# Reading the moving columns of a three-pass product in pairs, one from each half

## The chip, the cores and the metric

The kernel runs on one core of one Trainium2 chip. The metric is device time in microseconds (us), from the first to the last instruction of the program with what lies around it; less is better. The kernel before takes 2271.94 us as the median of three runs (2271.86 to 2279.43).

## The reference

A stack of four layers works on 256 tokens of width 1024, all in float32. Each layer is a half-step feed-forward block, a mixer and another half-step feed-forward block, each with an RMS norm before and after:

```python
for layer in range(DEPTH):
    g = norm_g[layer]
    h = swiglu_ffn(rms_norm(x, g[0]), ffn_w_gu[layer, 0], ffn_w_down[layer, 0])
    x = x + HALF_STEP * rms_norm(h, g[1])
    h = rms_norm(x, g[2])
    # layer % 3: 0 mLSTM, 1 RWKV-7, 2 retention; layers 0 and 3 are mLSTM
    h = mixer(h)
    x = x + rms_norm(h, g[3])
    h = swiglu_ffn(rms_norm(x, g[4]), ffn_w_gu[layer, 1], ffn_w_down[layer, 1])
    x = x + HALF_STEP * rms_norm(h, g[5])
```

`swiglu_ffn` is `(silu(x @ w_gate) * (x @ w_up)) @ w_down` with an inner width of 2816. Nearly all of the arithmetic is in its eight calls; the mixers add input products of 1024 x 3072 (mLSTM), 3 x 1024 x 1024 (RWKV) and 1024 x 6144 (retention), their output products, and their own recurrences in chunks.

## The kernel before, in words

The weights stream in as units of 128 x 2048 float32 (1 MB), in the order in which the products use them, all issued on SyncE's queue (`dma`). Each unit is split into a high and a low part both in float32r: ScalarE writes `hi` (L127), VectorE, or GpSimd in the mixers, writes `lo = raw - hi` (L135). Activations are split in the same way. A product is then three matmuls per block of 128 rows, high x high, high x low and low x high, summed in PSUM. The function `mm3` (L323) issues them, and it has two forms, after which operand moves through the array while the other is loaded into it as 128 x 128 weights:

- `w_moves=True` (L326 to L328): the weights move and the activations of 128 tokens are loaded. The result has tokens in its partitions and weight columns along the free dimension. The heads of all stages use it with 256 moving columns (`proj_B`, L349), so do the v, o and g products of the mixers, and the down and output products with 512 moving columns (`down_steps`, L376).
- `w_moves=False` (L330 to L332): the activations move, all 256 tokens of one block of 128 rows, and a block of 128 weight columns is loaded. The result is transposed: channels in the partitions, tokens along the free dimension. `proj_A` (L358) uses it for the feed-forward units after the head, `proj_qk` for the q and k of retention, `dense` of the mLSTM stage for its q and k, and `proj_unit` (L1446) of the RWKV stage for r and k.

In both forms the moving columns are read one after the other, as they lie in SBUF.

A feed-forward stage has 22 units of gate and up columns (each holds 128 gate and the 128 up columns of the same channels) and 11 of down rows. Its first three units are the head, computed token tile by token tile together with the end of the stage before; the other 19 go through `proj_A`, 48 matmuls of 256 columns each, and `evac_A` (L541). That function multiplies PSUM by the row of norm factors R (VectorE, L546), takes Silu of the gate half (ScalarE, L548), multiplies (VectorE, L549) and splits the result (L346, L347). After every second unit the down product of the chunk before runs, 24 matmuls of 512 columns, into four PSUM banks that hold the sum over the whole stage. Four further PSUM banks rotate for everything else. In these stages the order of the instructions is that of the code.

In the mLSTM and RWKV stages a planner (`Plan`) orders the instructions: each chain of steps yields an engine and an assumed cost in ns, and the planner issues what can start first on its clock. The retention stage is written out by hand. The lines that evacuate products of the second form there are L826 (mLSTM, times R), L1127 to L1129 (retention, rotation of q and k by cosine and sine) and L1526 (RWKV, copy on ScalarE).

The host lays out the weights before the launch (`a8` and `d2` from L2170 on, and the functions that put a stage's units in order). This takes no device time.

Of the kernel before, what the change touches and what calls it, by code (L numbers as in the profile page):

```python
# [20 lines left out]
P = 128  # L21
T = 256
# [12 lines left out]
class Net:  # L35
# [284 lines left out]
        s.nc.vector.tensor_copy(s.R, pt[:, :T])  # L320


    def mm3(s, out, wh, wl, ah, al, first, last, w_moves):  # L323
        mm = s.nc.tensor.matmul
        if w_moves:
            mm(out, ah, wh, start=first, stop=False)  # L326
            mm(out, ah, wl, start=False, stop=False)  # L327
            mm(out, al, wh, start=False, stop=last)  # L328
        else:
            mm(out, wh, ah, start=first, stop=False)  # L330
            mm(out, wh, al, start=False, stop=False)  # L331
            mm(out, wl, ah, start=False, stop=last)  # L332
# [16 lines left out]
    def proj_B(s, ps, unit, t):  # L349
# [5 lines left out]
        for k in range(NK):  # L355
            s.mm3(ps, wh[:, k, :], wl[:, k, :], s.xh[:, k, c], s.xl[:, k, c], k == 0, k == NK - 1, True)

    def proj_A(s, ps, unit, between=None):  # L358

        hi, lo = unit  # L360
        wh = hi.rearrange("p (k c) -> p k c", k=NK)
        wl = lo.rearrange("p (k c) -> p k c", k=NK)
        for g in range(2):
            c = slice(g * P, (g + 1) * P)
            for k in range(NK):
                s.mm3(ps[:, g * T:(g + 1) * T], wh[:, k, c], wl[:, k, c], s.xh[:, k, :], s.xl[:, k, :],
                      k == 0, k == NK - 1, False)
            if g == 0 and between is not None:
                between()
# [124 lines left out]
class Ffn(Stage):  # L494
# [46 lines left out]
    def evac_A(s, ps, u):  # L541
        n, nc = s.n, s.n.nc
        gn = n.sc(2, [2, T])
        sg = n.sc(1, [T])
        h = n.sc(1, [T])
        nc.vector.tensor_tensor(out=gn, in0=ps.rearrange("p (g t) -> p g t", g=2),  # L546
                                in1=n.R[:, None, :].to_broadcast([P, 2, T]), op=ALU.mult)
        nc.scalar.activation(out=sg, in_=gn[:, 0, :], func=AF.Silu)  # L548
        nc.vector.tensor_tensor(out=h, in0=gn[:, 1, :], in1=sg, op=ALU.mult)  # L549
        n.split([a[:, u % 2, :] for a in s.hTs(u // 2)], h)  # L550
# [147 lines left out]
class Mlstm(Stage):  # L698
# [66 lines left out]
    def dense(s):  # L765

        n, nc = s.n, s.n.nc
        yield "pe", 3000.0, True
        s.gates()
        s.plan.mark("gates")  # L770
        for i, (what, h) in enumerate(s.ORDER):
            yield from s.need(i)
            hi, lo = [u.rearrange("p (k c) -> p k c", k=NK) for u in n.get()]
            for j in range(2):
                c = slice(j * P, (j + 1) * P)
                for k in range(NK):
                    if k % 4 == 0:
                        yield "pe", 1300.0, j + k == 0
                        if j + k == 0:
                            ps = n.mm()  # L780
                    first, last = k == 0, k == NK - 1
                    if what == "qk":
                        n.mm3(ps[:, j * T:(j + 1) * T], hi[:, k, c], lo[:, k, c], n.xh[:, k, :], n.xl[:, k, :], first, last, False)
                    else:
                        n.mm3(ps[:, j * T:(j + 1) * T], hi[:, k, :], lo[:, k, :], n.xh[:, k, c], n.xl[:, k, c], first, last, True)
            n.free()
            s.ps[what, h] = ps.rearrange("p (g t) -> p g t", g=2)
            s.plan.mark("ps", what, h)
        yield from s.need(len(s.ORDER))
        yield [("y", 0), ("y", 1), ("hT", 0)]  # L790
        u = n.get()
        for t in range(2):
            if t == 0:
                n.load_gpost(s.gi)
                s.acc = n.new_acc()
            yield from n.down_steps(u, s.hT[0], t, s.acc[t], True, False)
        n.free()
# [20 lines left out]
    def conv(s):  # L818

        n, nc = s.n, s.n.nc  # L820
        for h in range(s.H):
            yield [("ps", "qk", h)]
            yield "ve", 600.0
            x = n.sc(4, [2, T + 3])
            nc.gpsimd.memset(x[:, :, 0:3], 0.0)
            nc.vector.tensor_tensor(out=x[:, :, 3:], in0=s.ps.pop(("qk", h)), in1=n.R[:, None, :].to_broadcast([P, 2, T]), op=ALU.mult)  # L826
            s.plan.drop()
            yield "po", 2220.0
            c = n.sc(4, [2, T])
            for g in range(2):  # L830
                nc.gpsimd.tensor_scalar(out=c[:, g, :], in0=x[:, g, 3:3 + T], scalar1=s.cw[:, 4 * g + h, 3:4], scalar2=None, op0=ALU.mult)
            for j in (2, 1, 0):
                yield "ve", 900.0
                for g in range(2):
                    nc.vector.scalar_tensor_tensor(out=c[:, g, :], in0=x[:, g, j:j + T], scalar=s.cw[:, 4 * g + h, j:j + 1],
                                                   in1=c[:, g, :], op0=ALU.mult, op1=ALU.add)
            yield "ac", 520.0, "sigmoid"
            sg = x[:, :, 0:T]
            nc.scalar.activation(out=sg, in_=c, func=AF.Sigmoid)
            yield "ve", 600.0  # L840
            s.qk[h] = n.sc(2, [2, T])
            nc.vector.tensor_tensor(out=s.qk[h], in0=c, in1=sg, op=ALU.mult)
            s.plan.mark("qk", h)

    def gates(s):
        n, nc = s.n, s.n.nc
        s.psg = n.mm()
        for k in range(NK):
            n.mm3(s.psg[0:36, 0:T], s.wgh[0][:, k, :], s.wgh[1][:, k, :], n.xh[:, k, :], n.xl[:, k, :], k == 0, k == NK - 1, False)
        n.make_R()  # L850

    def gates2(s):
# [190 lines left out]
class Retention(Stage):  # L1043
# [73 lines left out]
    def proj_qk(s, which, h):  # L1117
# [4 lines left out]
        if s.cos is not None and not hasattr(s, "nsin"):  # L1122
            n.make_R()
            s.rope()
        pv = ps.rearrange("p (g t) -> p g t", g=2)
        r, w = n.sc(2, [2, T]), n.sc(2, [2, T])
        nc.vector.tensor_tensor(out=r, in0=pv, in1=s.cos[:, None, :].to_broadcast([P, 2, T]), op=ALU.mult)  # L1127
        nc.vector.tensor_tensor(out=w[:, 0, :], in0=pv[:, 1, :], in1=s.nsin, op=ALU.mult)
        nc.vector.tensor_tensor(out=w[:, 1, :], in0=pv[:, 0, :], in1=s.sin, op=ALU.mult)  # L1129
        nc.gpsimd.tensor_tensor(out=r, in0=r, in1=w, op=ALU.add)  # L1130
        s.qk[which, h] = r
        n.ahead()
# [95 lines left out]
class Rwkv(Stage):  # L1228
# [200 lines left out]
                    s.plan.mark("ps", "v", i // 2, t)  # L1429
        s.plan.mark("V")  # L1430

    def unit(s):
        hi, lo = s.n.get()
        return hi.rearrange("p (k c) -> p k c", k=NK), lo.rearrange("p (k c) -> p k c", k=NK)

    def proj(s, hl, wh, wl, j, ps=None):

        for k in range(NK):
# [7 lines left out]
    def proj_unit(s, hl, name, g, j):  # L1446

        n = s.n
        yield from s.need(j)
        wh, wl = s.unit()  # L1450
        ps = None
        for j in range(2):
            c = slice(j * P, (j + 1) * P)
            ps = yield from s.proj(hl, wh[:, :, c], wl[:, :, c], j, ps)
        n.free()
        s.ps[name, g] = ps
        s.plan.mark("ps", name, g)
# [54 lines left out]
    def evacs(s):  # L1512
# [7 lines left out]
        for what in (("k", 0), ("k", 1), "la", "lg", ("r", 0), ("k", 2), ("k", 3), ("r", 1), ("r", 2), ("r", 3)):  # L1520
            if isinstance(what, tuple):
# [1 line left out]
                yield "ac", 500.0  # L1523
                store = s.kx if what[0] == "k" else s.r
                o = store[what[1]] = n.sc(2, [2, T])
                nc.scalar.activation(out=o.rearrange("p a b -> p (a b)"), in_=s.ps[what], func=AF.Copy)  # L1526
                s.plan.drop()
                s.plan.mark(*what)
                continue
# [82 lines left out]
    def lora2(s, i):  # L1612
# [6 lines left out]
        for g in range(4):  # L1619
            yield "pe", 640.0, True  # L1620
            ps = n.mm()
            for j in range(2):
                c = slice(D + (2 * g + j) * P, D + (2 * g + j + 1) * P)
                n.mm3(ps[:, j * T:(j + 1) * T], hi[rows, c], lo[rows, c], s.la[0][rows], s.la[1][rows], True, True, False)
            yield "ac", 620.0, "sigmoid"
            store[g] = n.sc(2, [2, T])
            for j in range(2):
# [5 lines left out]
    def lora2_g(s):  # L1633
# [4 lines left out]
        for t in range(2):  # L1638
            for h in range(2):
# [1 line left out]
                ps = n.mm()  # L1641
                c = slice(h * 512, h * 512 + 512)
                r = slice(t * P, (t + 1) * P)
                n.mm3(ps, hi[:, c], lo[:, c], s.lg[0][:, r], s.lg[1][:, r], True, True, True)
                yield "ac", 500.0
                nc.scalar.activation(out=s.G[:, t, c], in_=ps, func=AF.Copy)
                s.plan.drop()
# [525 lines left out]
    return m.reshape(NK, P, c, 256).transpose(2, 1, 0, 3).reshape(c, P, 2048)  # L2173


def d2(m):

    c = m.shape[0] // 256
    return m.reshape(c, 2, P, D).transpose(0, 2, 1, 3).reshape(c, P, 2048)


# [4 lines left out]

def ffn_units(gu, down, tail):
    g = gu.reshape(D, 2, DFF // P, P).transpose(0, 2, 1, 3).reshape(D, 2 * DFF)
    g, d = a8(g), d2(down)
    order = [g[0:2]]  # L2190
    for c in range(1, NCH):
        order.append(g[2 * c:2 * c + 2])
# [5 lines left out]

def mlstm_units(w_in, w_out):
    q, k, v, o = w_in[:, 0:512], w_in[:, 512:1024], w_in[:, 1024:2048], w_in[:, 2048:3072]  # L2200
    v, o, d = a8(v), a8(o), d2(w_out)
    qk = a8(np.stack([q.reshape(D, 4, P), k.reshape(D, 4, P)], axis=2).reshape(D, D))
    return np.stack([v[0], o[0], v[1], qk[0], qk[1], o[1], qk[2], o[2], qk[3], o[3], v[2], v[3], d[0], d[1], d[2], d[3]])


def ret_units(w_in, w_out):
    q, k, v, g, d = a8(w_in[:, 0:1024]), a8(w_in[:, 1024:2048]), a8(w_in[:, 2048:4096]), a8(w_in[:, 4096:6144]), d2(w_out)
    o = [v[0], v[1], g[0], q[0], k[0], g[1]]
    for h in (1, 2):
        o += [q[h], k[h], v[2 * h], v[2 * h + 1], g[2 * h], d[2 * h - 2], g[2 * h + 1], d[2 * h - 1]]  # L2210
# [2 lines left out]


def rwkv_units(w_rkv, w2, a2, g2, w_out):
    r, k, v = [a8(w_rkv[i]) for i in range(3)]
    l2 = np.concatenate([g2, np.concatenate([w2, a2], axis=0)], axis=1)[None]
    return np.concatenate([v, k[0:2], l2, r[0:1], k[2:4], r[1:4], d2(w_out)])

# [83 lines left out]
```

## Time and profile before

| | |
|---|---|
| median of three runs | 2271.94 us |
| lowest, highest | 2271.86, 2279.43 us |
| profiled execution, its own time | 2279.94 us |
| its span, first to last instruction | 2278.2 us |
| mean granted TensorE clock | 0.976 |
| instructions | 38723 |
| HBM read, written | 373.93 MB, 1.05 MB |

The profile names engines PE (TensorE's matmuls), PEld (its weight loads, which overlap the matmuls), DVE (VectorE), ACT (ScalarE), POOL (GpSimd) and SP (SyncE). A group of instructions stands as line, engine, operation, output<-inputs, shapes and count, then the busy time in us, the mean of one in ns, and the idle time of the engine just before them with what ended it. In a row of the timeline the first number is the start in us and the second how long the row's instructions took, first start to last end. A matmul's time runs from its start until its result is out, so it overlaps the next; its pace is the distance from start to start. In a table of windows each engine has its busy us and the number of instructions, then come the granted clock, the share of the DMA engines and GB/s. PSUM tiles are called mm (the rotating banks) and acc (the sums), SBUF scratch tiles s and q.

### The profile page before, as it was taken

The page shows a single profiled execution, that of the slowest core. Times are in us where ns is not written, and L with a number is a line of the kernel's source. Part 1 is how long each engine was busy: PE and PEld are TensorE (multiplying, and loading weights), DVE is VectorE, ACT ScalarE, POOL GpSimd, SP SyncE. Part 2 cuts the span into 40 slices and gives each one's busy share as a digit, 9 for nine tenths or more (in the row PEclk, how much of TensorE's full clock was granted, in tenths as well). Part 3 has the DMA queues.
Part 4 walks back from the last instruction along what each step waited for, and adds up shares of the span by engine and source line. Part 5 has one row for each costly group of instructions (what it writes and reads, how often), then busy time and mean ns, then how long its engine had stood idle before and what let it go on. Part 6 is the DMA issues. An engine that isn't in the chain of part 4 may idle for free.

```text
span 2278.2 us, 38723 instructions
## 1 busy us (share of the span) xinstructions
PE 2186.6 (96%) x16056; PEld 2029.7 (89%) x16056; DVE 1523.0 (67%) x2203; ACT 1099.3 (48%) x1742; POOL 469.2 (21%) x693
## 2 busy tenths in 40 slices
PE   8999989999997789989999999999999999998998
PEld 8999869999996678879999999998999999987997
DVE  6666777667669664777667667556766766677765
ACT  5445655445444353525445445444544544564543
POOL 1002840002006564641001002111100100383000
PEclk9999999999998897989999999999999999999999
DMA  7543336545551221125554554543555555333651
GB/s 282 207 182 130 130 139 245 189 168 223 188 183 59 90 75 47 57 93 213 200 189 187 196 195 176 192 167 139 213 202 186 188 204 189 126 140 142 233 195 69
DMA packets 55792, 377.48 MB, mean 166 GB/s; under 512 B 6840, under 2 KB 8504, under 8 KB 11328
## 3 DMA queue, kind: packets, MB, share of 16 engines
q1 hardware_dynamic: 55040, 373.63, 45.3%
q8 instruction: 126, 2.06, 0.4%
q10 hardware_dynamic: 576, 1.38, 0.2%
q14 instruction: 50, 0.41, 0.1%
HBM read 373.93 MB, written 1.05 MB: 165 GB/s over the span
## 4 chain that ended last, share of the span: by engine, by line
PE 84%; DVE 8%; POOL 3%; issue 2%; ACT 1%; DMA 1%; DVEq 0%; ACTq 0%; POOLq 0%; SPq 0%
PE mm L330 14%; PE mm L332 14%; PE mm L331 14%; PE acc L328 8%; PE acc L327 8%; PE acc L326 8%; PE mm L326 4%; PE mm L327 4%; PE mm L328 4%; POOL lo L135 1%; DVE lo L135 1%; PE mm L292 1%; PE mm L1925 1%; PE mm L1882 1%; DVE q L1337 1%
## 5 line engine op out<-in xcount | busy, mean ns | idle before, releaser
L135 DVE TENSOR_TENSOR lo<-raw,hi 128x1024 fp32r<-128x1024 f32 (+1 forms) x673 | 791.6, 1219 | 215.5 <-ACT hi L127 212.8
L127 ACT ACTIVATE hi<-raw 128x1024 fp32r<-128x1024 f32 (+1 forms) x772 | 698.4, 959 | 137.6 <-issue 80.9
L330 PE MATMUL mm<-xh,hi 128*128 128x256 f32 x2688 | 746.2, 278 | 0.0
L332 PE MATMUL mm<-xh,lo 128*128 128x256 f32 x2688 | 744.4, 277 | 0.7 <-DVE lo L135 0.7
L331 PE MATMUL mm<-xl,hi 128*128 128x256 f32 x2688 | 744.4, 277 | 0.0
L331 PEld LDWEIGHTS mm<-xl,hi 128*128 128x128 f32 x2688 | 504.9, 188 | 2.7
L330 PEld LDWEIGHTS mm<-xh,hi 128*128 128x128 f32 x2688 | 504.9, 188 | 2.7
L332 PEld LDWEIGHTS mm<-xh,lo 128*128 128x128 f32 x2688 | 505.9, 188 | 1.1 <-DVE lo L135 1.1
L328 PE MATMUL acc<-hi,s 128*128 128x512 f32 x864 | 344.1, 398 | 13.7 <-DVE s L347 9.9
L326 PE MATMUL acc<-hi,s 128*128 128x512 f32 x864 | 343.5, 398 | 5.0 <-ACT s L346 4.5
L327 PE MATMUL acc<-lo,s 128*128 128x512 f32 x864 | 341.5, 395 | 0.0
L326 PE MATMUL mm<-hi,xh 128*128 128x256 f32 x960 | 274.5, 286 | 10.1 <-ACT xh L1342 10.1
L548 ACT ACTIVATE s<-s 128x256 f32<-128x256 f32 x152 | 63.5, 418 | 448.1 <-DVE s L546 448.1
L328 PE MATMUL mm<-hi,xl 128*128 128x256 f32 x960 | 270.2, 281 | 3.2 <-DVE xl L1344 3.2
L327 PE MATMUL mm<-lo,xh 128*128 128x256 f32 x960 | 270.3, 282 | 0.0
L252 POOL TENSOR_SCALAR rr_v<-ssx 128x1 f32<-128x1 f32 x22 | 5.2, 234 | 1181.5 <-ACT junk L307 1181.5
L328 PEld LDWEIGHTS acc<-hi,s 128*128 128x128 f32 x864 | 164.4, 190 | 51.2 <-DVE s L347 12.3
L326 PEld LDWEIGHTS acc<-hi,s 128*128 128x128 f32 x864 | 164.2, 190 | 38.5 <-ACT s L346 5.9
L327 PEld LDWEIGHTS acc<-lo,s 128*128 128x128 f32 x864 | 164.2, 190 | 33.4
L326 PEld LDWEIGHTS mm<-hi,xh 128*128 128x128 f32 x960 | 182.6, 190 | 12.1 <-ACT xh L1342 10.6
L135 POOL TENSOR_TENSOR lo<-raw,hi 128x512 fp32r<-128x512 f32 x99 | 140.5, 1431 | 231.6 <-ACT hi L127 231.5
L328 PEld LDWEIGHTS mm<-hi,xl 128*128 128x128 f32 x960 | 181.9, 189 | 4.2 <-DVE xl L1344 3.8
(414 smaller groups left out, 2441.4 us busy)
## 6 DMA issues: line engine op xcount, KB each, us to landing
raw<-in_w SPq DMA_DIRECT2D x345, 1024.0 KB, 4.8
s<-in_g_post SPq DMA_DIRECT2D x12, 512.0 KB, 6.3
x<-in_x ACTq DMA_DIRECT2D x2, 512.0 KB, 5.7
s<-in_ml_g SPq DMA_DIRECT2D x2, 512.0 KB, 6.7
q<-in_rw_l SPq DMA_DIRECT2D x1, 1024.0 KB
s<-in_rw_ln SPq DMA_DIRECT2D x8, 128.0 KB, 4.9
out<-x SPq DMA_DIRECT2D x3, 256.0 KB, 2.1
s<-in_decay SPq DMA_DIRECT2D x1, 512.0 KB, 5.9
```

Of the source, the lines that this page charges most:

```text
L127: s.nc.scalar.activation(out=o[0], in_=src, func=AF.Copy)
L135: (e or s.nc.vector).tensor_tensor(out=o[1], in0=src, in1=o[0].bitcast(F32), op=ALU.subtract)
L292: nc.tensor.transpose(pt[:, q * P:(q + 1) * P], s.x[t][:, k * P:(k + 1) * P], s.ident)
L326: mm(out, ah, wh, start=first, stop=False)
L327: mm(out, ah, wl, start=False, stop=False)
L328: mm(out, al, wh, start=False, stop=last)
L330: mm(out, wh, ah, start=first, stop=False)
L331: mm(out, wh, al, start=False, stop=False)
L332: mm(out, wl, ah, start=False, stop=last)
L548: nc.scalar.activation(out=sg, in_=gn[:, 0, :], func=AF.Silu)
L1337: nc.vector.scalar_tensor_tensor(out=raw()[:, q], in0=s.xx[h][:, q, c], scalar=s.mu[:, i, 4 * h + q:4 * h + q + 1], in1=s.xn[h][:, q, c], ...
L1882: nc.tensor.matmul(ps[:, b, ct, :], v[lhs][r, ct, c, :], v["rt"][r, ct, c, :], start=True, stop=True)
```

## The change

`mm3` gets an argument `pairs`, true unless a caller says otherwise. With it the moving operand is read in another order: column 0, column n/2, column 1, column n/2 + 1, and so on, where n is 256 or 512. The output is written without a break, in the order of reading, and the matmuls keep their number, shapes and order.

```diff
-    def mm3(s, out, wh, wl, ah, al, first, last, w_moves):
+    def mm3(s, out, wh, wl, ah, al, first, last, w_moves, pairs=True):
         mm = s.nc.tensor.matmul
+        if pairs:
+            out = out.rearrange("p (b a) -> p b a", a=2)
+            by2 = lambda x: x.rearrange("p (a b) -> p b a", a=2)
+            if w_moves:
+                wh, wl = by2(wh), by2(wl)
+            else:
+                ah, al = by2(ah), by2(al)
         if w_moves:
             mm(out, ah, wh, start=first, stop=False)
```

Where the weights move, the host has laid the even columns of each group first and then the odd ones, so that the result comes out in the old order: groups of 256 columns in `units_B`, which takes the place of `a8` for the heads of the feed-forward stages and for v, o and g of the mixers, and groups of 512 in `d2`.

```diff
+def units_B(m):
+    c = m.shape[1] // 256
+    return a8(m.reshape(D, c, P, 2).transpose(0, 1, 3, 2).reshape(D, -1))
...
 def d2(m):
     c = m.shape[0] // 256
+    m = m.reshape(-1, 2, 256, 2).transpose(0, 1, 3, 2)
     return m.reshape(c, 2, P, D).transpose(0, 2, 1, 3).reshape(c, P, 2048)
```

Where the activations move, their layout stays, so the result lies in PSUM with tokens 0, 128, 1, 129, ... next to each other. The evacuation undoes that: it reads PSUM through `tokens`, with every second element, and writes the old order to SBUF. This is done in `evac_A` (L546), in the mLSTM `conv` (L826), in `proj_qk` (L1127 to L1129) and in the RWKV `evacs` (L1526).

```diff
+    def tokens(ps):
+        return ps.rearrange("p (g b a) -> p g a b", g=2, a=2)
...
-        nc.vector.tensor_tensor(out=gn, in0=ps.rearrange("p (g t) -> p g t", g=2),
-                                in1=n.R[:, None, :].to_broadcast([P, 2, T]), op=ALU.mult)
+        nc.vector.tensor_tensor(out=gn.rearrange("p g (a b) -> p g a b", a=2), in0=n.tokens(ps),
+                                in1=n.R.rearrange("p (a b) -> p a b", a=2)[:, None].to_broadcast([P, 2, 2, P]), op=ALU.mult)
...
-                nc.scalar.activation(out=o.rearrange("p a b -> p (a b)"), in_=s.ps[what], func=AF.Copy)
+                nc.scalar.activation(out=o.rearrange("p g (a b) -> p g a b", a=2), in_=n.tokens(s.ps[what]), func=AF.Copy)
```

Three callers pass `pairs=False` and stay as they were: the mLSTM gates (36 weight columns), and the two second LoRA products of the RWKV stage (L1612, L1633). `blocks_A` takes over the slicing of a unit into its two blocks of 128 columns, with the same addresses as before. The planner's costs are not changed.

More of the change, by code (lines that the diff above doesn't have):

```diff
@@ L356, in proj_B, with blocks_A @@
             s.mm3(ps, wh[:, k, :], wl[:, k, :], s.xh[:, k, c], s.xl[:, k, c], k == 0, k == NK - 1, True)
-    def proj_A(s, ps, unit, between=None):
[L360 to L364, printed above, removed]
+    @staticmethod
+    def blocks_A(unit):
+        v = [x.rearrange("p (k g b) -> p k g b", k=NK, g=2) for x in unit]
+        return [[x[:, :, g] for x in v] for g in range(2)]
+    @staticmethod
+    def tokens(ps):
+        return ps.rearrange("p (g b a) -> p g a b", g=2, a=2)
+    def proj_A(s, ps, unit, between=None):
+        for g, (wh, wl) in enumerate(s.blocks_A(unit)):
             for k in range(NK):
-                s.mm3(ps[:, g * T:(g + 1) * T], wh[:, k, c], wl[:, k, c], s.xh[:, k, :], s.xl[:, k, :],
+                s.mm3(ps[:, g * T:(g + 1) * T], wh[:, k], wl[:, k], s.xh[:, k, :], s.xl[:, k, :],
                       k == 0, k == NK - 1, False)
@@ L772, in dense @@
             yield from s.need(i)
-            hi, lo = [u.rearrange("p (k c) -> p k c", k=NK) for u in n.get()]
+            u = n.get()
+            hi, lo = [x.rearrange("p (k c) -> p k c", k=NK) for x in u]
+            blocks = n.blocks_A(u)
             for j in range(2):
@@ L782, in dense @@
                     if what == "qk":
-                        n.mm3(ps[:, j * T:(j + 1) * T], hi[:, k, c], lo[:, k, c], n.xh[:, k, :], n.xl[:, k, :], first, last, False)
+                        n.mm3(ps[:, j * T:(j + 1) * T], blocks[j][0][:, k], blocks[j][1][:, k], n.xh[:, k, :], n.xl[:, k, :], first, last, False)
                     else:
@@ L786, in dense @@
             n.free()
-            s.ps[what, h] = ps.rearrange("p (g t) -> p g t", g=2)
+            s.ps[what, h] = n.tokens(ps) if what == "qk" else ps.rearrange("p (g t) -> p g t", g=2)
             s.plan.mark("ps", what, h)
@@ L825, in conv @@
             nc.gpsimd.memset(x[:, :, 0:3], 0.0)
-            nc.vector.tensor_tensor(out=x[:, :, 3:], in0=s.ps.pop(("qk", h)), in1=n.R[:, None, :].to_broadcast([P, 2, T]), op=ALU.mult)
+            nc.vector.tensor_tensor(out=x[:, :, 3:].rearrange("p g (a b) -> p g a b", a=2), in0=s.ps.pop(("qk", h)),
+                                    in1=n.R.rearrange("p (a b) -> p a b", a=2)[:, None].to_broadcast([P, 2, 2, P]), op=ALU.mult)
             s.plan.drop()
@@ L848, in gates @@
         for k in range(NK):
-            n.mm3(s.psg[0:36, 0:T], s.wgh[0][:, k, :], s.wgh[1][:, k, :], n.xh[:, k, :], n.xl[:, k, :], k == 0, k == NK - 1, False)
+            n.mm3(s.psg[0:36, 0:T], s.wgh[0][:, k, :], s.wgh[1][:, k, :], n.xh[:, k, :], n.xl[:, k, :], k == 0, k == NK - 1, False, False)
         n.make_R()
@@ L1124, in proj_qk @@
             s.rope()
-        pv = ps.rearrange("p (g t) -> p g t", g=2)
+        pv = n.tokens(ps)
         r, w = n.sc(2, [2, T]), n.sc(2, [2, T])
-        nc.vector.tensor_tensor(out=r, in0=pv, in1=s.cos[:, None, :].to_broadcast([P, 2, T]), op=ALU.mult)
-        nc.vector.tensor_tensor(out=w[:, 0, :], in0=pv[:, 1, :], in1=s.nsin, op=ALU.mult)
-        nc.vector.tensor_tensor(out=w[:, 1, :], in0=pv[:, 0, :], in1=s.sin, op=ALU.mult)
+        by2 = lambda x: x.rearrange("p (a b) -> p a b", a=2)
+        nc.vector.tensor_tensor(out=r.rearrange("p g (a b) -> p g a b", a=2), in0=pv, in1=by2(s.cos)[:, None].to_broadcast([P, 2, 2, P]), op=ALU.mult)
+        nc.vector.tensor_tensor(out=by2(w[:, 0, :]), in0=pv[:, 1], in1=by2(s.nsin), op=ALU.mult)
+        nc.vector.tensor_tensor(out=by2(w[:, 1, :]), in0=pv[:, 0], in1=by2(s.sin), op=ALU.mult)
         nc.gpsimd.tensor_tensor(out=r, in0=r, in1=w, op=ALU.add)
@@ L1430, in values @@
         s.plan.mark("V")
-    def unit(s):
-        hi, lo = s.n.get()
-        return hi.rearrange("p (k c) -> p k c", k=NK), lo.rearrange("p (k c) -> p k c", k=NK)
     def proj(s, hl, wh, wl, j, ps=None):
@@ L1449, in proj_unit @@
         yield from s.need(j)
-        wh, wl = s.unit()
         ps = None
-        for j in range(2):
-            c = slice(j * P, (j + 1) * P)
-            ps = yield from s.proj(hl, wh[:, :, c], wl[:, :, c], j, ps)
+        for j, (wh, wl) in enumerate(n.blocks_A(n.get())):
+            ps = yield from s.proj(hl, wh, wl, j, ps)
         n.free()
@@ L1623, in lora2 @@
                 c = slice(D + (2 * g + j) * P, D + (2 * g + j + 1) * P)
-                n.mm3(ps[:, j * T:(j + 1) * T], hi[rows, c], lo[rows, c], s.la[0][rows], s.la[1][rows], True, True, False)
+                n.mm3(ps[:, j * T:(j + 1) * T], hi[rows, c], lo[rows, c], s.la[0][rows], s.la[1][rows], True, True, False, False)
             yield "ac", 620.0, "sigmoid"
@@ L1643, in lora2_g @@
                 r = slice(t * P, (t + 1) * P)
-                n.mm3(ps, hi[:, c], lo[:, c], s.lg[0][:, r], s.lg[1][:, r], True, True, True)
+                n.mm3(ps, hi[:, c], lo[:, c], s.lg[0][:, r], s.lg[1][:, r], True, True, True, False)
                 yield "ac", 500.0
@@ L2188, in ffn_units @@
     g = gu.reshape(D, 2, DFF // P, P).transpose(0, 2, 1, 3).reshape(D, 2 * DFF)
-    g, d = a8(g), d2(down)
+    g, d = np.concatenate([units_B(g[:, :NHEAD * 256]), a8(g[:, NHEAD * 256:])]), d2(down)
     order = [g[0:2]]
@@ L2200, in mlstm_units @@
     q, k, v, o = w_in[:, 0:512], w_in[:, 512:1024], w_in[:, 1024:2048], w_in[:, 2048:3072]
-    v, o, d = a8(v), a8(o), d2(w_out)
+    v, o, d = units_B(v), units_B(o), d2(w_out)
     qk = a8(np.stack([q.reshape(D, 4, P), k.reshape(D, 4, P)], axis=2).reshape(D, D))
@@ L2206, in ret_units @@
 def ret_units(w_in, w_out):
-    q, k, v, g, d = a8(w_in[:, 0:1024]), a8(w_in[:, 1024:2048]), a8(w_in[:, 2048:4096]), a8(w_in[:, 4096:6144]), d2(w_out)
+    q, k = a8(w_in[:, 0:1024]), a8(w_in[:, 1024:2048])
+    v, g, d = units_B(w_in[:, 2048:4096]), units_B(w_in[:, 4096:6144]), d2(w_out)
     o = [v[0], v[1], g[0], q[0], k[0], g[1]]
@@ L2215, in rwkv_units @@
 def rwkv_units(w_rkv, w2, a2, g2, w_out):
-    r, k, v = [a8(w_rkv[i]) for i in range(3)]
+    r, k, v = a8(w_rkv[0]), a8(w_rkv[1]), units_B(w_rkv[2])
     l2 = np.concatenate([g2, np.concatenate([w2, a2], axis=0)], axis=1)[None]
```

## The prediction

> **What bounds the kernel now.** I read the page first, for its shares and its chain.
>
> ```profile
> span 2278.2 us, 38723 instructions
> ...
> PE 2186.6 (96%) x16056; PEld 2029.7 (89%) x16056; DVE 1523.0 (67%) x2203; ACT 1099.3 (48%) x1742; POOL 469.2 (21%) x693
> ...
> PE 84%; DVE 8%; POOL 3%; issue 2%; ACT 1%; DMA 1%; DVEq 0%; ACTq 0%; POOLq 0%; SPq 0%
> ...
> PE mm L330 14%; PE mm L332 14%; PE mm L331 14%; PE acc L328 8%; PE acc L327 8%; PE acc L326 8%; PE mm L326 4%; PE mm L327 4%; PE mm L328 4%; POOL lo L135 1%; DVE lo L135 1%; PE mm L292 1%; PE mm L1925 1%; PE mm L1882 1%; DVE q L1337 1%
> ```
>
> The chain of work that ended last is TensorE for 84% of the span, and the six lines of mm3 alone (L326 to L332) are 3x14 + 3x8 + 3x4 = 78% of it, or 1777 us. These are the matmuls that the change touches. The windows of two feed-forward interiors show how tight that is:
>
> ```profile
> core 0: us, PE busy (x) PEld busy (x) DVE busy (x) ACT busy (x) POOL busy (x), PEclk, DMA share, GB/s
> 36.00:176.00 140.00, 140.00 (x1011) 132.05 (x1010) 90.46 (x109) 65.33 (x88) 0.00 (x0) 1.00 0.59 215
> 345.00:490.00 145.00, 145.00 (x1083) 137.09 (x1083) 94.24 (x113) 69.32 (x93) 0.00 (x0) 1.00 0.58 214
> ```
>
> TensorE has no gap, its granted clock is 1.00, VectorE is at 94 of 145 us and the DMA engines are at 0.58. So here the time is the pace of the matmuls. The pace isn't the duration of one, since they overlap; it is read from start to start, in the timeline:
>
> ```profile
> 125.01 0.28 PE L330 MATMUL mm<-xh,hi 128*128 128x256 f32 x1
> ...
> 136.32 0.40 PE L326 MATMUL acc<-hi,s 128*128 128x512 f32 x1
> ...
> 141.83 0.28 PE L330 MATMUL mm<-xh,hi 128*128 128x256 f32 x1
> ...
> 413.33 0.28 PE L330 MATMUL mm<-xh,hi 128*128 128x256 f32 x1
> ...
> 414.35 0.28 PE L330 MATMUL mm<-xh,hi 128*128 128x256 f32 x1
> ...
> 1428.38 1.02 PE L1139 MATMUL mm<-s,s 128*128 128x256 f32 x4
> 1429.24 0.61 PE L1141 MATMUL mm<-s,s 128*128 128x128 f32 x4
> ...
> 945.15 1.06 PE L1975 MATMUL mm<-q,s 128*128 128x64 f32 x8
> 946.04 1.06 PE L1978 MATMUL mm<-s,s 128*128 128x64 f32 x8
> ```
>
> Between 125.01 and 136.32 lie two units of proj_A, 96 matmuls of 256 columns: 11.31 / 96 = 117.8 ns each. Then come the 24 matmuls of 512 columns of one down unit: 5.51 / 24 = 229.6 ns. In another feed-forward stage nine of 256 columns take 1.02 us, 113.3 ns each: the same instructions at another level. So a matmul of 256 columns is at 113.3 or 117.8 ns, one of 512 at 229.6.
>
> The last four rows give the two floors. L1139 is a plain fp32 product of 256 columns with the same 128x128 weights: 0.86 us for four, 215 ns. L1975 has 64 columns and a 128x128 weight load for each: 0.89 us for eight, 111 ns; the columns can't be its limit, so I take 111 ns as the pace of the weight loads, which no three-pass matmul can go below.
>
> **Where the loss is that the change can reach.** These groups, with shapes kept apart, have the counts and the means:
>
> ```profile
> L330 PE MATMUL mm<-xh,hi 128*128 128x256 f32 x2688 | 746.2, 278 | 0.0
> ...
> L331 PE MATMUL mm<-xl,hi 128*128 128x256 f32 x2688 | 744.4, 277 | 0.0
> ...
> L327 PE MATMUL acc<-lo,s 128*128 128x512 f32 x864 | 341.5, 395 | 0.0
> ...
> L327 PE MATMUL mm<-lo,xh 128*128 128x256 f32 x960 | 270.3, 282 | 0.0
> ...
> L330 PE MATMUL mm<-q,hi 128*128 128x256 f32 x128 | 42.4, 331 | 0.7 <-ACT s L1867 0.7
> ...
> L1139 PE MATMUL mm<-s,s 128*128 128x256 f32 x16 | 4.1, 378 | 0.0
> ...
> L1152 PE MATMUL mm<-s,s 128*128 128x512 f32 x24 | 11.0, 592 | 0.0
> ...
> L1843 PE MATMUL acc<-gx,s 128*128 128x64 f16 x128 | 10.2, 209 | 0.5 <-ACT gx L1846 0.4 <-DVE s L1837 0.2
> ...
> L1933 PE MATMUL mm<-s,q 128*128 128x64 bf16 x64 | 4.9, 202 | 0.0
> ```
>
> Plain fp32 goes from 378 to 592 ns when 256 columns are added, 214 ns, as much as its pace of 215. The three-pass matmuls go from 277 to 395, 118 ns, for the same 256. So plain fp32 takes about two steps for each column and the three-pass one takes one. Then L1139 (256 columns) and a three-pass matmul of 512 make the same number of steps behind the same weight load, and still one costs 215 and the other 229.6. What differs is that the second has to fetch a new column at every step. I conclude that 14.6 ns of each matmul of 512 columns are lost in fetching the moving operand, at full rate, beside a weight load; and the change alters nothing else on TensorE than the order of that fetch.
>
> **The change part by part.**
>
> The matmuls keep their number, sizes and order. Those changed: of 256 columns with the activations moving 3 x (2688 + 128) = 8448, with the weights moving 3 x 960 = 2880, and 3 x 864 = 2592 of 512. The first group's pace: its mean is 277 to 278 ns, and these two windows calibrate it:
>
> ```profile
> L330 PE MATMUL mm<-xh,hi 128*128 128x256 f32 x116 | 32.1, 276 | 0.0
> ...
> L332 PE MATMUL mm<-xh,lo 128*128 128x256 f32 x151 | 42.4, 281 | 0.0
> ```
>
> A mean of 276 is that of the stage at 113.3 (window 420 to 480), 281 that of the stage at 117.8 (100 to 175), so 277 to 278 is about 114.5. The second group's 282 is 118. Together the three groups take 8448 x 114.5 + 2880 x 118 + 2592 x 229.6 = 967 + 340 + 595 = 1902 us of pace, of which the chain holds 1777, or 0.93: a nanosecond saved is worth 0.93 at the end, since the RWKV stage and the stage boundaries wait for other engines.
>
> The most that a better order can give is the distance to the floors: 8448 x (114.5 - 111) = 29.6 us, 2880 x (118 - 111) = 20.2, 2592 x (229.6 - 215) = 37.8; together 87.6, times 0.93, 81 us. The least within this case is nothing. No matmul in the trace alternates between two places column by column, so nothing shows how much of the loss goes. I take half, 41 us: two levels, 113.3 and 117.8, for the same instructions say that the loss hangs on how the fetches fall, and that at its better level a matmul of 256 columns is already within 2.3 ns of the floor, while the 512 ones are never near theirs.
>
> What the other engines pay: results of the products with moving activations now lie in PSUM in pair order, and whoever evacuates them reads every second element. DMA issues, their sizes and their queues stay the same; the host's order costs no device time. No wait is added and no instruction moves in a queue.
>
> ```profile
> L546 DVE TENSOR_TENSOR s<-mm,R 128x512 f32<-128x512 f32 x152 | 104.8, 689 | 96.4 <-PE mm L332 94.6
> ...
> L826 DVE TENSOR_TENSOR s<-mm,R 128x512 f32<-128x512 f32 x8 | 5.5, 688 | 8.4 <-POOL s L825 6.2 <-PE mm L332 2.2
> ...
> L1127 DVE TENSOR_TENSOR s<-mm,s 128x512 f32<-128x512 f32 x8 | 5.5, 689 | 10.4 <-PE mm L332 10.4
> ...
> L1526 ACT ACTIVATE s<-mm x8: 577/597/597, 752.4 to 936.1; 128x512 f32<-128x512 f32 x8
> ...
> L1831 DVE TENSOR_TENSOR s<-acc,rw_zm 128x256 f16<-128x256 f32 x16 | 6.6, 417 | 5.7 <-PE acc L1828 4.7 <-ACT gx L1852 1.0
> ...
> L1929 DVE TENSOR_TENSOR s<-mm,s 128x256 bf16<-128x256 f32 x16 | 6.7, 420 | 17.2 <-PE mm L1925 11.9 <-POOL s L1927 4.2 <-PE acc L1811 0.6
> ```
>
> The nearest row of a broken-up pattern is L1831, which writes its result in blocks: 417 ns, against 420 for the unbroken L1929. So I take zero. The upper bound is that each doubles. For the 152 evacuations of the feed-forward stages that is 0.69 us each, one per unit of 48 x 0.1133 = 5.4 us: at most 145 / 5.4 x 0.69 = 19 us on top of VectorE's 94 in a window of 145, so TensorE, with four PSUM banks ahead, still covers it; without that cover it would be 105 us. In the mixers, where less covers it, the bound is 8 x 0.69 (L826) + 8 x 0.69 (L1127) + 8 x 0.60 (L1526) and as much again as L1127 for the two half-size products after it: 21 us if all of it were exposed.
>
> Sum: 41 us off. The profiled execution took 2279.94 us, so 2239 in its terms; the three timed runs have their median 8 us lower, at 2271.94, and there I forecast 2231.
>
> **The rivals.**
>
> The first is *half rate*. Each column of a pair comes from another place, and if the fetch gains from neighbours, splitting them costs a step each. What it would make is the plain fp32 rows: 215 ns for 256 columns, and for 512 the 592-ns group, whose pace is 592 - (378 - 215) = 429. That is 8448 x 100.5 + 2880 x 97 + 2592 x 199.4 = 849 + 279 + 517 = 1645 us more, 3917 us. It decides early: there are 11328 x 128 + 2592 x 256 = 2.1 million pairs, so 0.02 ns on each pair (of 229.6 / 256 = 0.9 now) eats the forecast gain. For it: the fetch at full rate is what already loses time. Against it: L1843 reads its 64 columns in runs of 8 to 64 with gaps between (the even and odd blocks of the inverse), and takes 209 ns against 202 for the unbroken L1933, so a jump costs little there; but these runs have at least eight neighbours. [...]
>
> The second is *no change*: the loss belongs to the handover between a weight load and its matmul and not to the order of the columns. For it: the levels 113.3 and 117.8 differ without any change of the operands' order, and most matmuls of 256 columns stand near the weight loads' 111 anyway. Against it: a handover would cost L1139 the same, and that has no loss. It gives 2272, or up to 2293 with the 21 us of the evacuations.
>
> **How the numbers follow.** Gain 0.64, no change 0.16, half rate or a milder slowing 0.20. The gain case runs from 81 us off (2191) to the least that can be told from nothing: a measurement of this kernel resolves about 0.5%, 11 us (2261). The range takes in the no-change case with its evacuation bound, 2293, and leaves out half rate, which is 2 in 10. So faster by over 0.5% has 0.64, within it 0.16, slower 0.20.
>
> **What would show it.** If right: the 512-column rows start every 215 to 225 ns and their mean falls from 395 to 381 to 390, the 256-column ones lie under 113.3 everywhere, the 117.8 level is gone, and L546 stays near 689. If the fetch isn't the cause, the mean durations of L326 to L332 stand still. If the half-rate rival holds, 395 becomes about 592 and 277 about 378. The forecast is also wrong if the matmuls gain and VectorE then shows as the releaser of the down products, L546 having doubled.

## The result and the profile after

The changed kernel takes 2215.72 us (median of four runs, 2208.96 to 2218.86) against 2275.16 for the kernel before in four runs. The ratio is 0.9734, with a 95% interval of 0.9701 to 0.9766: 59 us less. The profiled execution took 2213.64 us, 66 less than that of before.

The page of the changed kernel, busy shares and chain:

```profile
span 2211.9 us, 38741 instructions
...
PE 2108.9 (95%) x16056; PEld 1989.0 (90%) x16056; DVE 1519.9 (69%) x2203; ACT 1097.5 (50%) x1742; POOL 468.8 (21%) x693
...
PE 78%; DVE 13%; POOL 4%; issue 3%; ACT 2%; DMA 0%; DVEq 0%; SPq 0%; POOLq 0%; ACTq 0%
PE mm L338 14%; PE mm L339 14%; PE mm L340 14%; PE acc L336 7%; PE acc L334 7%; PE acc L335 7%; PE mm L336 3%; PE mm L334 3%; PE mm L335 3%; DVE lo L135 2%; POOL lo L135 1%; DVE s L270 1%; DVE x L276 1%; ACT hi L127 1%; PE mm L1895 1%
```

Count and work are the same (16056 matmuls, VectorE busy 1520 us against 1523). The six lines of mm3, now L334 to L340, hold 72% of the chain instead of 78%, and VectorE's share has gone from 8% to 13%.

The timeline of a feed-forward interior, from the middle of a train of 256-column matmuls through one down unit:

```profile
387.79 0.28 PE L338 MATMUL mm<-xh,hi 128*128 128x256 f32 x1
...
390.81 0.38 PE L334 MATMUL acc<-hi,s 128*128 128x512 f32 x1
...
395.99 0.27 PE L338 MATMUL mm<-xh,hi 128*128 128x256 f32 x1
```

27 matmuls of 256 columns take 3.02 us, 111.9 ns each; the 24 of 512 columns take 5.18, 215.8 ns each. Before it was 113.3 or 117.8, and 229.6. The groups say the same of the whole program, with shapes kept apart:

```profile
L338 PE MATMUL mm<-xh,hi 128*128 128x256 f32 x2688 | 741.1, 276 | 0.0
...
L335 PE MATMUL acc<-lo,s 128*128 128x512 f32 x864 | 329.7, 382 | 0.0
...
L335 PE MATMUL mm<-lo,xh 128*128 128x256 f32 x960 | 266.0, 277 | 0.0
```

The 512-column group went from 395 to 382 ns, the 256-column group with moving weights from 282 to 277. The evacuations with every second element (VectorE in the feed-forward, mLSTM and retention stages, then ScalarE in RWKV):

```profile
L561 DVE TENSOR_TENSOR s<-mm,R 128x512 f32<-128x512 f32 x152 | 104.7, 689 | 82.9 <-PE mm L340 82.9
...
L1146 DVE TENSOR_TENSOR s<-mm,s 128x512 f32<-128x512 f32 x8 | 5.5, 689 | 8.7 <-PE mm L340 8.7
...
L843 DVE TENSOR_TENSOR s<-mm,R 128x512 f32<-128x512 f32 x8 | 5.5, 688 | 8.3 <-POOL s L842 6.3 <-PE mm L340 2.0
```

```profile
L1539 ACT ACTIVATE s<-mm x8: 572/597/598, 734.4 to 909.2; 128x512 f32<-128x512 f32 x8
```

They take 689, 689, 688 and 597 ns (the last one a median), what L546, L1127, L826 and L1526 took before. Reading PSUM with every second element costs nothing measurable here.

### The profile page after: what moved, and what is told of

Read it like the earlier page. It is cut to its first block, busy times and chain, and to the rows that moved or that the text cites. A ratio compares the mean times of both kernels' runs of the same rounds, so it can differ in the third digit from the quotient of the medians.

```text
span 2211.9 us, 38741 instructions
## 1 busy us (share of the span) xinstructions
PE 2108.9 (95%) x16056; PEld 1989.0 (90%) x16056; DVE 1519.9 (69%) x2203; ACT 1097.5 (50%) x1742; POOL 468.8 (21%) x693
## 4 chain that ended last, share of the span: by engine, by line
PE 78%; DVE 13%; POOL 4%; issue 3%; ACT 2%; DMA 0%; DVEq 0%; SPq 0%; POOLq 0%; ACTq 0%
PE mm L338 14%; PE mm L339 14%; PE mm L340 14%; PE acc L336 7%; PE acc L334 7%; PE acc L335 7%; PE mm L336 3%; PE mm L334 3%; PE mm L335 3%; DVE lo L135 2%; POOL lo L135 1%; DVE s L270 1%; DVE x L276 1%; ACT hi L127 1%; PE mm L1895 1%
## 5 line engine op out<-in xcount | busy, mean ns | idle before, releaser
L340 PE MATMUL mm<-xh,lo 128*128 128x256 f32 x2688 | 740.0, 275 | 0.9 <-DVE lo L135 0.9
L339 PEld LDWEIGHTS mm<-xl,hi 128*128 128x128 f32 x2688 | 516.5, 192 | 1.7
L338 PEld LDWEIGHTS mm<-xh,hi 128*128 128x128 f32 x2688 | 516.4, 192 | 1.7
L340 PEld LDWEIGHTS mm<-xh,lo 128*128 128x128 f32 x2688 | 516.6, 192 | 1.3 <-DVE lo L135 1.3
L336 PE MATMUL acc<-hi,s 128*128 128x512 f32 x864 | 331.3, 383 | 14.5 <-DVE s L355 10.2
L334 PE MATMUL acc<-hi,s 128*128 128x512 f32 x864 | 333.4, 386 | 5.0 <-ACT s L354 4.5
L335 PE MATMUL acc<-lo,s 128*128 128x512 f32 x864 | 329.7, 382 | 0.0
L334 PE MATMUL mm<-hi,xh 128*128 128x256 f32 x960 | 270.5, 282 | 12.0 <-ACT xh L1361 12.0
L334 PEld LDWEIGHTS mm<-hi,xh 128*128 128x128 f32 x960 | 186.3, 194 | 13.7 <-ACT xh L1361 12.4
L334 PEld LDWEIGHTS acc<-hi,s 128*128 128x128 f32 x864 | 165.2, 191 | 27.5 <-ACT s L354 5.9
L335 PEld LDWEIGHTS mm<-lo,xh 128*128 128x128 f32 x960 | 186.3, 194 | 1.3 <-issue 1.0
```

## The experiments

### Which part brings what

Three kernels each keep the pairs for one of the three kinds of product; the other two kinds are read in order, with their old layouts.

```diff
-        if pairs:
+        kind = "A" if not w_moves else "D" if wh.shape[-1] == 512 else "B"
+        if pairs and kind in "D":
             out = out.rearrange("p (b a) -> p b a", a=2)
```

The kernel above pairs the 512 columns alone ("D"). The other two have "A" (moving activations) or "B" (256 columns with moving weights) in its place.

> Only the products of 512 moving columns (down and output products) read in pairs; all others read in order, with their old layouts. By the paces, 229.6 to 216 ns on 2592 matmuls, of which 0.93 counts: 33 us less than before, ratio 0.986. If these matmuls were hidden behind something else, less.

> Only the products whose activations move (8448 matmuls of 256 columns, with the evacuation that undoes the order) read in pairs. By the paces, 114.5 to 112 ns: 20 us less, ratio 0.991. If the evacuations or the weight loads take it back, near 1.

> Only the products whose weights move in 256 columns (2880 matmuls, heads and v, o, g) read in pairs. By the paces, 118 to 112 ns: 16 us less, ratio 0.993. Together the three parts make 69 us if they add up, against 60 to 66 measured for all three at once.

Measured: only 512 columns 2263.49 us, ratio 0.9949 (0.9930 to 0.9969); only moving activations 2256.50, ratio 0.9907 (0.9883 to 0.9930); only 256 columns with moving weights 2269.70, ratio 0.9981 (0.9963 to 1.0000). The kernel before had 2274.83 beside them. The three gains make 11 + 18 + 5 = 34 us by the medians, not 60, and the interval of the last one reaches 1. The activations gave about what the paces say, the other two too little, the 512 columns only a third. The 256 columns with moving weights do start every 111.7 ns in the trace of their kernel (117.4 before), and the retention stage shows it, 4.4 us in the table below; where the rest of the expected 16 us stayed was not traced.

The trace of the kernel with only the 512 columns in pairs tells where much of it went. Two windows of it, one chunk apart, in the same feed-forward stage. From 352 to 363 us:

```profile
L339 PE MATMUL mm<-xh,hi 128*128 128x256 f32 x28 | 7.7, 276 | 0.0
...
L335 PE MATMUL acc<-hi,s 128*128 128x512 f32 x3 | 1.1, 379 | 0.0
```

And from 368 to 379.5 us:

```profile
L339 PE MATMUL mm<-xh,hi 128*128 128x256 f32 x28 | 7.9, 281 | 0.0
...
L337 PE MATMUL acc<-hi,s 128*128 128x512 f32 x4 | 1.5, 379 | 0.0
```

The 512-column matmuls are at 379 ns, their full gain, in both windows. But the train of 256-column matmuls, read in order, is at 276 in one chunk and at 281 in the next: the two levels of the prediction, 113.3 and 117.8, which alternate here from chunk to chunk, where the kernel before had the better one throughout this stage. By the starts, 4586 of the 8314 closely packed matmuls with moving activations are at 116 ns or more in this kernel, against 1725 of 8315 before: 13 us of pace given back, somewhat over half of the 22 that are missing from the expected 33. The rest was not traced to a place. To test the levels, the next kernel reads the activations and the 512 columns in pairs, so that the activations have no levels any more.

> The products with moving activations and those of 512 columns read in pairs, those of 256 columns with moving weights in order. The parts by themselves gave 11 us (512), 21 (activations) and 4 (256 with moving weights), 37 together, where all three at once give 60. Theory 1: the 512 part lost most of its gain because the products of 256 columns after it, read in order, fell to their slower level of 118 ns in every other chunk; with the activations in pairs that level is gone, so this kernel shows nearly the sum of the paces: 33 us for the 512 columns on top of the 21, ratio 0.976 to 0.978. Theory 2: the parts overlap with other waits and simply add: 32 us, ratio 0.986.

Measured: 2222.68 us, ratio 0.9777 (0.9756 to 0.9797), 53 us less. Theory 1 holds; the 0.986 of theory 2 lies outside the interval. On top of the activations the 512 columns bring 34 us by the medians and 30 by the ratios, where alone they brought 11. Stage by stage, as distances between the ends of the last residual updates in the traces:

| us | before | only 512 | only activations | only 256, moving weights | all but these | all |
|---|---|---|---|---|---|---|
| first feed-forward of layer 0 | 204.7 | 200.7 | 200.4 | 204.3 | 195.9 | 196.2 |
| second feed-forward of layer 0 | 184.0 | 183.0 | 182.3 | 183.4 | 179.2 | 178.6 |
| RWKV | 313.2 | 309.4 | 305.6 | 311.0 | 306.8 | 301.7 |
| retention | 201.1 | 198.8 | 199.5 | 196.7 | 197.4 | 193.0 |

In the second feed-forward stage, where the level fell in every other chunk, the 512 columns save 1.0 us alone and 3.1 beside the paired activations. In the first the same edit moved the level the other way: all its trains of 96 and 192 matmuls stood at 117.8 ns before, and every other one is at 113.4 in the kernel with only the 512 columns; there they save 4.0 alone and 4.5 in company. In retention, where the mean pace of the trains stays (115.7 and 115.8), they save 2.3 and 2.1. So of these three stages the one in which the level fell is the one in which the 512 columns come short. The RWKV row says little about it, since the granted clock of that stage differs as well (0.87 before, 0.90 in the changed kernel, 0.88 in the kernel of this test).

What sets the level was not found. In the trace of the kernel before, a train of in-order matmuls holds one level through 96 and more matmuls, up to 384 (at 113.4 ns on average, from 624.7 us), in the first feed-forward stage the worse one, 117.8, and the level changes there only where another kind of matmul or a wait comes between. The trains of r and k in its RWKV stage stand at a third level, 120 ns, at a granted clock of 1.00 (750.5 to 758 us).

### Does the loss need the weight load?

The changed kernel with one product more in pairs: the mLSTM gates, 256 moving columns against weights of 36 columns instead of 128. Their evacuation undoes the order.

```diff
-            n.mm3(s.psg[0:36, 0:T], s.wgh[0][:, k, :], s.wgh[1][:, k, :], n.xh[:, k, :], n.xl[:, k, :], k == 0, k == NK - 1, False, False)
+            n.mm3(s.psg[0:36, 0:T], s.wgh[0][:, k, :], s.wgh[1][:, k, :], n.xh[:, k, :], n.xl[:, k, :], k == 0, k == NK - 1, False)
```

> The changed kernel with the mLSTM gates read in pairs too: 256 moving columns against weights of only 36 columns. In order, these 48 matmuls start every 117 to 118 ns in the kernels before and after. If the loss belongs to the fetch of the moving columns alone, they fall to about 109 ns, and the 112 ns that the other products of 256 columns now show is then the pace of loading 128 weight columns. If the loss needs a full weight load beside it, they had nothing to lose and stay at 117 to 118. If 112 is a floor of the moving side, they fall to 112 and no further.

The timeline of the kernel before, 24 gates in order, first and last:

```profile
216.61 0.28 PE L330 MATMUL mm<-xh,s 128*36 128x256 f32 x1
...
219.32 0.28 PE L332 MATMUL mm<-xh,s 128*36 128x256 f32 x1
```

And of the experiment:

```profile
207.59 0.27 PE L338 MATMUL mm<-xh,s 128*36 128x256 f32 x1
...
210.10 0.27 PE L340 MATMUL mm<-xh,s 128*36 128x256 f32 x1
```

23 steps in 2.71 us are 117.8 ns, in 2.51 they are 109.1. So the loss of 8 to 9 ns is there without a full weight load, and it goes with the order of the moving columns. And with pairs and 36 weight columns the pace goes below the 112 ns of the products with 128, so what is left of those, 111.9 less 109.1 or 2 to 3 ns, goes with the number of their weight columns, as the prediction took it. Time of the kernel: 2215.18 us in one run, no different from the changed kernel; the 48 matmuls are too few to show.

### Which orders are fast?

In each of three kernels the eight feed-forward stages read the 512 moving columns of their down products in eight different orders; the host lays the weights to match. All other products are read in pairs.

```diff
+PATS = [('c', 'c', {}), ('ab', 'ba', {'a': 2}), ('cab', 'cba', {'a': 2, 'b': 4}), ('cab', 'cba', {'a': 2, 'b': 16}), ('cab', 'cba', {'a': 2, 'b': 64}), ('ba', 'ab', {'a': 2}), ('ab', 'ba', {'a': 4}), ('abe', 'bae', {'a': 2, 'e': 2})]
...
+            src, dst, kw = PATS[pat]
...
+            view = lambda x: x.rearrange(f"p ({' '.join(src)}) -> p {' '.join(dst)}", **kw)
+            wh, wl = view(wh), view(wl)
```

`pat` is the number of the feed-forward stage, and each entry of `PATS` gives the layout of the columns and the order in which they are read; the list above is that of the first kernel.

> Each of the eight feed-forward stages reads the 512 moving columns of its down products in another order (the host lays the weights to match, so the outputs stay): 1 one after the other; 2 pairs, one of each half; 3 pairs 4 columns apart; 4 pairs 16 columns apart; 5 pairs 64 columns apart; 6 all even columns, then all odd ones; 7 fours, one of each quarter; 8 two neighbours of one half, then two of the other. All other products read in pairs of halves. Theory 1, what pays is that successive columns come from different places: stages 2, 3, 4, 5 and 7 start a matmul every 216 ns, stage 1 every 229 ns, 6 and 8 lie between. Theory 2, what pays is the distance of the two places: 216 ns only in 2, 7 and 8, and 3 is at 229 or above. Theory 3, the loss comes with neighbours read right after each other, wherever the next one lies: 6 is also at 216, 8 is at 229. Theory 4, a place must be hit more than once in a row to be read at full rate: 2, 3, 4, 5 and 7 should be slow, which the changed kernel already speaks against for 2; a stage far above 229 would show it for another distance.

> A second set of reading orders for the 512 moving columns of the down products, one for each feed-forward stage (the outputs stay the same): 1 pairs two columns apart (0, 2, 1, 3, ...); 2 in order, but written as an access pattern of two levels; 3 four neighbours of one half, then four of the other; 4 the same with eight; 5 eights, one of each eighth; 6 every fourth column, in four passes; 7 pairs of halves, first all even columns, then all odd ones; 8 pairs of halves, every fourth column, in four passes. The first set gave 216 ns for pairs 4, 16, 64 and 256 columns apart, 453 for even-then-odd, 279 for fours, 340 for couples, 231 in order. If what counts is that a step from column to column neither stays in the same four columns nor goes on in one direction inside them, 1 is slow (near 453), 7 and 8 are at 216. If what counts is the shape of the pattern, an innermost level of two, then 1, 7 and 8 are all at 216. If neighbouring reads of the same four columns help as long as they come soon, 8 is slower than 7 and 7 slower than 216. For long runs I expect 3 and 4 between 340 and 231, falling with the length; 5 above 279; 6 at 453 or above.

> A third set of orders, to test a reckoning from the first two sets: columns lie in groups of four; a round of the fetch takes 1.8 ns, brings the new groups that two successive reads ask for, and the columns of a group already brought are free; a matmul takes its rounds or 216 ns, whichever is more. In order, 512 columns are 128 rounds (230 ns), pairs 64 (hidden), even-then-odd 256 (460). Feed-forward stages: 1, 2 and 3 are pairs 8, 32 and 128 columns apart: 216. 5 every 8th column in eight passes and 6 every 32nd: 512 new groups, two a round, 256 rounds, 453 to 461. 7 sixteens, one of each sixteenth: 256 rounds if sixteen groups aren't kept, 460 to 490 as with eights. 4 fours that lie 4 columns apart (0, 4, 8, 12, 1, ...): 64 rounds and 216 by the reckoning if four groups are kept; the fours of quarters gave 279, which the reckoning misses, so 279 here says that it is the number of groups in use and not their distance. 8 fours two apart (0, 2, 4, 6, 1, 3, 5, 7): two groups in use, each brought by itself, 128 rounds, 231. The rival reckoning, that places far enough apart are what pays, makes 1 slower than 3.

The three kernels took 2331.32, 2437.28 and 2436.03 us in one run each. Measured in their traces, as the median distance of the starts in each stage:

| order of the 512 columns | ns |
|---|---|
| in order; the same in two levels | 231; 231 |
| pairs 4, 8, 16, 32, 64, 128, 256 columns apart | 216 each |
| pairs 2 columns apart (0, 2, 1, 3) | 232 |
| pairs of halves, evens then odds (0, 256, 2, 258) | 231 |
| pairs of halves, every fourth column (0, 256, 4, 260) | 453 |
| all evens, then all odds (0, 2, 4) | 453 |
| every fourth column; every eighth; every 32nd | 461; 431; 433 |
| fours, from four quarters; four columns apart | 279; 268 |
| fours two columns apart (0, 2, 4, 6, 1, 3, 5, 7) | 340 |
| couples of neighbours, of either half in turn | 340 |
| runs of four, of eight, of either half in turn | 252; 245 |
| eights, one of each eighth; sixteens | 487; 433 |

Five rows of the first of these kernels, groups of the down products in the windows of their stages (in order, pairs 16 apart, evens then odds, fours, couples):

```profile
L352 PE MATMUL acc<-lo,s 128*128 128x512 f32 x82 | 32.3, 394 | 0.0
...
L352 PE MATMUL acc<-lo,s 128*128 128x512 f32 x81 | 30.7, 379 | 0.0
...
L352 PE MATMUL acc<-lo,s 128*128 128x512 f32 x84 | 54.0, 642 | 0.0
...
L352 PE MATMUL acc<-lo,s 128*128 128x512 f32 x83 | 36.7, 442 | 0.0
...
L352 PE MATMUL acc<-lo,s 128*128 128x512 f32 x83 | 42.1, 507 | 0.0
```

And the window of the stage with evens then odds:

```profile
1566.00:1783.00 217.00, 217.00 (x1174) 154.94 (x1174) 106.77 (x135) 77.01 (x105) 0.00 (x0) 1.00 0.42 151
```

TensorE counts as busy in all of its 217 us at a granted clock of 1.00, and the weight loads fill only 155 of them. In order (the first stage, 30 to 188 us) the same count was 158 of 158 and 147. So TensorE is as full as before and the stage is longer for it, which the busy share alone doesn't tell.

What follows. The distance of a pair makes no difference from 4 columns to 256, 216 ns each, so it isn't the halves that pay. Pairs 2 apart give nothing, 232 ns against 231 in order, from which I infer groups of four columns; no trace shows the groups themselves. And pairs of halves are at 216 if the next pair stays in the same two groups; with evens first they are at 231, with every fourth column at 453. So all four theories of the first set, and in the second set the two that put it down to the step between columns or to the shape of the pattern, all fall; the third of the second set, that reads of one group must follow soon, is the one that stands (231, then 453), though it doesn't say why in-order reading loses.

The reckoning of the third set is an estimate of mine, fitted to the paces of the first two: it supposes rounds of 1.8 ns, which is the in-order 230 ns over 128 groups of four, and that a round brings the new groups that two successive reads ask for. No trace shows a round. By the estimate, reading in order would take one round for four columns, which at the pace of the pairs are worth 216 / 512 x 4 = 1.69 ns, so the round would be the longer by a little, 128 x 1.8 = 230; in pairs a round would bring two groups, eight columns, and be hidden. It fits the in-order rows, all pairs, evens then odds and every fourth column. Of the orders of the third kernel it had pairs 8, 32 and 128 apart right and missed the others: every eighth and every 32nd column gave 431 and 433 for 453 to 461, the sixteens 433 for 460 to 490, the fours 268 and 340 for 216 and 231. Couples and runs don't fit either. So it is a summary of reading in one or two streams, argued and not shown; why reading in order loses, and how three or more places are served, stays open. The rival reckoning, that a greater distance helps, is refuted: 8, 32 and 128 apart are the same.

Two rows speak most against theory 4 of the first set: pairs of halves, whose successive reads are 256 columns apart, run at 216, and evens then odds, which read two columns of every four one right after the other, at 453.

## Why the prediction was right, and where it missed

**Direction and place.** The chain was TensorE's and the pace of the mm3 lines was the time. The result came through that pace: the work of the other engines stayed the same.

**The loss in the fetch.** Plain fp32 at 215 ns for 256 columns pointed to 14.6 ns lost on 512 columns, which the prediction put down not to the steps or the weight load but to fetching a new column at every step. The changed kernel, whose matmuls differ in the order of reading alone, gets back 13.8 of them. The addition "beside a weight load" was too narrow: the gates lose 8 to 9 ns with weights of 36 columns. A matmul that loses it with no weight load at all was not run.

**The floors.** 215 and 111 were forecast as bounds, 215.8 and 111.9 measured. The gates, at 109 with 36 weight columns, show that the last 2 to 3 ns of the 256-column matmuls go with their 128 weight columns. But 111 ns is not the pace of every load of 128 columns. The transposes of L292, in the kernel before, load 128x128 weights for each matmul too:

```profile
508.99 1.04 PE L292 MATMUL mm<-ident,x 128*128 128x128 f32 x8
...
L292 PEld LDWEIGHTS mm<-ident,x x176: 138/141/231, 4.7 to 2093.2; 128*128 128x128 f32 x176
```

By the starts they follow each other every 109 ns (median), and their loads take 141 ns where those of L330 take 188. The bound held for the three-pass matmuls; what makes their loads longer is open.

**The size.** The step that failed is "I take half". Of 87.6 us between the paces and the floors, 8448 x (114.5 - 111.9) + 2880 x (118 - 111.9) + 2592 x (229.6 - 215.8) = 22.0 + 17.6 + 35.8 = 75 us are gone, all but the last nanosecond of each matmul. The argument for half was that the two levels show that the loss hangs on how the fetches fall, and that the better level is near the floor; but both levels belong to reading in order, and say nothing of an order without the loss. No row showed such an order, so half was a guess. The one row without the loss, L1139, served as the bound, and the paces came within a nanosecond of it: the forecast 41 us off became 59 by the medians and 66 in the profiled executions.

**The weight at the end.** 0.93 was reckoned from the chain. 59 of 75 by the medians is 0.79; the 66 of the profiled executions would be 0.88, but 11.5 of them lie in the RWKV stage, where the granted clock was 0.87 before and 0.90 after. The two mLSTM stages gave next to nothing, 130.0 and 129.8 us before, 129.1 and 130.0 after, though the pace of their matmuls fell too, with 512 columns from 231 to 216 ns (median). The chain after has more of VectorE (13% instead of 8%), which fits waits that TensorE used to cover and that have come to light; this was not tested.

**The evacuations.** Zero was taken and is what was measured, row by row: 689, 689, 688 and 597 ns, before and after.

**The rivals.** *Half rate* is a real effect: evens then odds, read so in one stage alone, take 453 ns and lengthen that stage from 178.7 to 240.2 us. The prediction had priced it at 429. But it showed only in strides, in pairs that step on by four columns, and in eights and sixteens; pairs that stay in their two groups of four until these are used up don't have it. *No change*, with the loss in the handover from weight load to matmul, falls with the gates, which keep the handover and lose the loss. Its argument, the two levels, is a fact, and in the kernel that paired the 512 columns alone the worse level took 13 us back.

## What to carry to other kernels

Where matmuls of float32r are packed and start further apart than a floor in the same trace, try reading the moving operand in pairs from two places at least four columns apart, both of which go on in order. Here that took 512 columns from 229.6 to 215.8 ns, and 256 from 113.3 or 117.8 to 111.9. The host's order is made before the launch, and the evacuations that undid the order took 689, 689, 688 and 597 ns as before. Take the floor from a row of the same trace that shows it: here 215 ns (L1139), which I took for as many steps without the loss, and 111 (L1975) for matmuls that load 128x128 weights each. And when a part brings too little by itself, look at the pace of the products beside it before discarding it: 11 us alone were 30 to 34 in company.

## What the runs showed that was not expected

Reading 512 float32r columns takes 216 ns in pairs at least four columns apart that go on column by column, 231 in order, and 431 to 487 in strides of 2 to 32 columns, in pairs of halves that step on by four, and in eights and sixteens; runs, fours and couples lie between, at 245 to 340. Outside the RWKV stage a train of in-order matmuls of 256 columns keeps one of two paces, 113.3 or 117.8 ns, until something interrupts it. With the moving columns in pairs, weights of 36 columns instead of 128 let a matmul of 256 columns start every 109 ns instead of 112.
